# FP32 decoder trunk on one core: the down projection's residual added by accumulating transfers, its subtractions and first evictions on other engines, and the last norm in a written order

## The chip, the cores and the metric

The kernel runs on one core of one Trainium2 chip. The metric is the device time of one execution in microseconds; the number given is the median of three runs. Every text below says TensorE for the matrix engine, VectorE (DVE in the rows), ScalarE (ACT), GpSimd (POOL) and SyncE (SP, which only starts transfers).

## What is computed

A two-layer decoder trunk over 1024 tokens of width 1024, in float32: one recurrent layer, one sparse-attention layer, each followed by a gated feed-forward part, and a last norm. Cut to what the change touches:

```python
def rmsnorm(x, g):
    y = x * lax.rsqrt(jnp.mean(x * x, axis=-1, keepdims=True) + EPS)
    return y * g

def swiglu(h, w_gu, w_down):
    u = h @ w_gu                      # 1024 -> 2 * 2816
    return (jax.nn.silu(u[..., :D_FF]) * u[..., D_FF:]) @ w_down

for layer in range(2):
    h = h + mixer(rmsnorm(h, norm_g[layer, 0]))
    h = h + swiglu(rmsnorm(h, norm_g[layer, 1]), w_gu[layer], w_down[layer])
return rmsnorm(h, final_g)
```

## The kernel before, in words

Activations are held transposed: eight tiles h[0] to h[7] of 128 features by 1024 tokens. Every float32 product is made of three products of split operands: a number is split into a rounded high part (ScalarE copy, L231) and the rest (VectorE subtraction, L232), and high x high, high x low and low x high are summed in PSUM. So each operand of TensorE costs one ScalarE and one VectorE operation before it can be used.

The feed-forward part (`ffn`, L681) multiplies 2x2 blocks with seven block products in place of eight (a Strassen-like scheme); sums of blocks of weights are made by transfers that add into SBUF (`acc`, L189, issued on GpSimd's queue, L190), sums of activations by GpSimd subtractions. The gated part goes over a list `seq` of block products, 12 matmuls each, evicted by `evict`. The norm of its input is applied late: `rstd_a` (L270) gets the reciprocal root per token (matmul of the squares with ones, L274; a power on GpSimd, L279; small VectorE steps, L281 to L285; diagonal matrices `dg`, L298), called at i == 4; `rstd_b` (L304) spreads it over the partitions by a matmul with ones (prb, L310) and a ScalarE copy, called at i == 6. Evictions that need it are held back until then (`late`). Product 6 of the list writes bank b of column tile 0 and is evicted at L791; product 7 is the same for column tile 1; product 8 (block product 7 of tile 0) adds onto bank b of tile 0.

The down projection (`down`, L853, with `block_proj`, L932) runs over three groups of contraction tiles (`DG = [3, 4, 4]`), in each over the seven block products in the order 1, 5, 6, 3, 7, 4, 2 (the text calls them steps), and in each step over four output tiles p: 84 products of 9 or 12 matmuls (L1022). For each product a weight is split (`pump`, L997, up to six products ahead), for each step the operands of the next one are made from the z tiles (`xop`, L945: a GpSimd subtraction at L949 to L955 for steps 5, 6, 4 and 7, then a split), and each product is evicted by adding its bank onto a half of a tile of h on VectorE (L1028). The weights of steps 5, 6, 3 and 7 are made in place in one tile by successive accumulating transfers (`prep`, L967, L991). The tiles of h start as the residual, loaded from DRAM by SyncE, 512 KB each (`hload`, L866, asked for four products ahead).

In the last layer (`last`, `tail`) the squares are summed on GpSimd or VectorE (`sq`, L883), and the last norm (`finish`, L1080) is made for tokens 512 to 1023 while steps 4 and 2 of the last group run, then for tokens 0 to 255 and 256 to 511; for that the last step is cut into two halves of 256 tokens. The outputs are scaled by VectorE (L1092) and sent by ScalarE's and SyncE's queues (L1094).

Which instruction stands where on its engine is decided by the framework's planner, a list scheduler with a timing model of its own, by program order and by the raised priority of a few blocks (`high_priority`). A part under `manual_schedule` keeps the written order instead.

Of the kernel before, what the change touches and what calls it, by code (L numbers as in the profile page):

```python
# [67 lines left out]
class Trunk:  # L68
# [612 lines left out]
    def ffn(self, L, h, last=False):  # L681
# [171 lines left out]
    def down(self, L, hd, zd, zout, last):  # L853
# [12 lines left out]
        def hload(m):  # L866
            h[m] = self.slot("h")
            nc.sync.dma_start(h[m], hd[m])
# [29 lines left out]
        for j, p, c in pr:  # L898
            if last:
                for m, x in {3: ((p, hi),), 7: ((p + 4, hi),), 4: ((p + 4, q[0]), (p + 4, q[1]))}.get(j, ((p, c),) if c else ()):  # L900
                    with self.tc.high_priority(offset=PRIO if j == 2 else 0):
                        sq(m, x, nc.vector if j == 2 else nc.gpsimd)
# [2 lines left out]
                if j == 4 or c == q[0]:
                    next(fin, None)
                if (j, p, c) == (2, 3, q[0]):
                    for _ in fin:
                        pass
                    fin = self.finish(h, st.pop(0), 0, 256)  # L910
                    with self.tc.high_priority(offset=PRIO):
                        next(fin)
            else:
                for m, x in {3: ((p, hi),), 7: ((p + 4, hi),), 4: ((p + 4, lo),), 2: ((p, lo),)}.get(j, ()):
                    kv(m, x)
                if (j, p) == (4, 3):
                    self.ld, self.sp = LD, SP
                    self.wpump(self.wi + 4, self.wi + 2)
        if last:
            next(fin)  # L920
            next(fin)
            f1 = self.finish(h, st.pop(256), 256, 256)
            with self.tc.high_priority(offset=PRIO):
                next(f1)
            for f in (fin, f1):
                for _ in f:
                    pass
            yield h
        else:
            yield kv  # L930
# [1052 lines left out]
```

## Time and profile before

| | before |
|---|---|
| median of three runs | 2741.74 us (2738.09 to 2742.91) |
| the profiled execution's own time | 2742.32 us |
| its span, first to last instruction | 2740.6 us |
| mean granted TensorE clock | 0.988 of full |
| TensorE busy | 2658.2 us, 97% of the span |
| VectorE, ScalarE, GpSimd busy | 69%, 47%, 41% |
| down projection of layer 0, of layer 1 | about 905 to 1122 us, 2485 to 2722 us |

A row of the timeline reads: start in us, busy us, engine, line of the kernel, operation, written tile <- read tiles, shape, count; in brackets the idle time of that engine before it and what ended it. A row that stands for several instructions gives the time they were busy together.

### The profile page before, as it was taken

The page shows a single profiled execution, that of the slowest core. Times are in us where ns is not written, and L with a number is a line of the kernel's source. Part 1 is how long each engine was busy: PE and PEld are TensorE (multiplying, and loading weights), DVE is VectorE, ACT ScalarE, POOL GpSimd, SP SyncE. Part 2 cuts the span into 40 slices and gives each one's busy share as a digit, 9 for nine tenths or more (in the row PEclk, how much of TensorE's full clock was granted, in tenths as well). Part 3 has the DMA queues.
Part 4 walks back from the last instruction along what each step waited for, and adds up shares of the span by engine and source line. Part 5 has one row for each costly group of instructions (what it writes and reads, how often), then busy time and mean ns, then how long its engine had stood idle before and what let it go on. Part 6 is the DMA issues. An engine that isn't in the chain of part 4 may idle for free.

```text
span 2740.6 us, 36687 instructions
## 1 busy us (share of the span) xinstructions
PE 2658.2 (97%) x12650; PEld 2204.7 (80%) x12650; DVE 1892.1 (69%) x3641; ACT 1301.7 (47%) x2505; POOL 1120.5 (41%) x1102
## 2 busy tenths in 40 slices
PE   8989999999999999999999999999999999999997
PEld 6867888788888778888888878888887888887786
DVE  8655734755555898647647999999856545557997
ACT  4656622433223443424415888989934323223433
POOL 2431103444333555110004677777634434436552
PEclk9998999999999999999999999999999999999998
DMA  3323533466564975353485322221354666559761
GB/s 126 93 83 104 170 143 111 112 156 166 150 161 117 324 201 112 133 154 91 162 244 155 82 67 59 67 76 49 108 174 104 170 156 152 154 128 287 194 146 62
DMA packets 175178, 377.03 MB, mean 138 GB/s; under 512 B 16896, under 2 KB 66432, under 8 KB 174992
## 3 DMA queue, kind: packets, MB, share of 16 engines
q1 hardware_dynamic: 121232, 256.79, 28.8%
q0 software_dynamic: 51872, 115.43, 19.6%
q10 hardware_dynamic: 1888, 2.46, 0.2%
q8 instruction: 100, 1.64, 0.2%
q14 instruction: 86, 0.70, 0.1%
HBM read 289.68 MB, written 78.64 MB: 134 GB/s over the span
## 4 chain that ended last, share of the span: by engine, by line
PE 68%; DVE 13%; issue 4%; DMA 3%; ACT 2%; POOL 1%; POOLq 0%; DVEq 0%; SPq 0%; ACTq 0%
PE pb L777 13%; PE pc L777 8%; PE pa L777 8%; PE pn L239 7%; PE pU L1022 6%; PE psc L239 4%; PE po L239 4%; DVE so L232 3%; PE pt L1644 2%; PE py L239 2%; PE pV L1022 2%; PE pwo L1834 2%; PE pW L1022 1%; PE po L1682 1%; PE po L1683 1%
## 5 line engine op out<-in xcount | busy, mean ns | idle before, releaser
L232 DVE TENSOR_TENSOR so<-wr,so 128x512 fp32r<-128x512 f32 (+1 forms) x476 | 390.9, 851 | 55.2 <-ACT so L231 54.6
L231 ACT ACTIVATE so<-wr 128x512 fp32r<-128x512 f32 (+1 forms) x476 | 279.1, 611 | 247.1 <-DMA wr<-w_dn 114.3
L777 PE MATMUL pb<-so,so 128*128 128x512 f32 x1584 | 382.8, 392 | 0.7 <-DVE so L232 0.7
L777 PEld LDWEIGHTS pb<-so,so 128*128 128x128 f32 x1584 | 300.2, 190 | 63.6 <-DVE so L232 1.1
L777 PE MATMUL pa<-so,so 128*128 128x512 f32 x1056 | 254.2, 393 | 4.1 <-ACT ev L786 2.6
L777 PE MATMUL pc<-so,so 128*128 128x512 f32 x1056 | 255.6, 389 | 0.0
L190 POOL DMA_DIRECT2D wr<-w_gu x176 | 161.6, 1076 | 226.0 <-DVE so L232 178.9
L1022 PE MATMUL pU<-so,so 128*128 128x512 f32 x1056 | 245.4, 390 | 2.3 <-DVE so L232 2.3
L777 PEld LDWEIGHTS pa<-so,so 128*128 128x128 f32 x1056 | 199.5, 189 | 46.6 <-DVE so L232 2.7
L239 PE MATMUL psc<-kl,ql 96*128 96x512 f32 (+2 forms) x960 | 232.8, 368 | 2.1 <-DVE thl L232 1.2
L1022 PEld LDWEIGHTS pU<-so,so 128*128 128x128 f32 x1056 | 197.9, 188 | 45.3 <-DVE so L232 4.0
L777 PEld LDWEIGHTS pc<-so,so 128*128 128x128 f32 x1056 | 198.3, 188 | 41.1
L805 ACT ACTIVATE ev<-ev 128x512 f32<-128x512 f32 x44 | 27.8, 632 | 349.4 <-POOL ev L804 349.4
L239 PEld LDWEIGHTS psc<-kl,ql 96*128 96x128 f32 x960 | 164.1, 190 | 24.7 <-PE pt L1644 2.2
L190 POOL DMA_DIRECT2D wr<-w_dn x96 | 91.4, 1136 | 135.7 <-DVE so L232 46.1
L804 POOL TENSOR_TENSOR ev<-ev,rb 128x512 f32<-128x512 f32 x44 | 58.2, 1322 | 209.0 <-DVE ev L803 209.0
L232 DVE TENSOR_TENSOR wl<-wr,wh 128x1024 fp32r<-128x1024 f32 (+4 forms) x79 | 87.8, 1127 | 77.5 <-ACT wh L231 53.2
L232 DVE TENSOR_TENSOR thl<-pt,thl 128x512 fp32r<-128x512 f32 x198 | 133.0, 681 | 10.3 <-ACT thl L231 10.1
L1022 PE MATMUL pV<-so,so 128*128 128x512 f32 x528 | 125.0, 392 | 8.6 <-DVE so L232 6.0
L231 ACT ACTIVATE wh<-wr 128x1024 fp32r<-128x1024 f32 (+4 forms) x97 | 90.1, 956 | 77.6 <-DMA wr<-w_q 19.7
L1022 PEld LDWEIGHTS pV<-so,so 128*128 128x128 f32 x528 | 98.2, 188 | 33.4 <-DVE so L232 7.7
L231 ACT ACTIVATE thl<-pt 128x512 fp32r<-128x512 f32 x198 | 114.5, 597 | 20.2 <-PE pt L1644 18.8
(331 smaller groups left out, 6366.7 us busy)
## 6 DMA issues: line engine op xcount, KB each, us to landing
wr<-w_gu SPq DMA_DIRECT2D x110, 512.0 KB, 4.8
wr<-w_gu POOLq DMA_DIRECT2D x176, 256.0 KB, 5.1
zd<-ev SPq DMA_DIRECT2D x44, 512.0 KB, 3.2
zr<-zd SPq DMA_DIRECT2D x44, 512.0 KB, 6.3
wr<-w_dn SPq DMA_DIRECT2D x40, 512.0 KB, 7.2
wr<-w_dn POOLq DMA_DIRECT2D x64, 256.0 KB, 5.1
ql<-qd SPq DMA_DIRECT2D x64, 192.0 KB, 3.1
wr<-w_in SPq DMA_DIRECT2D x23, 512.0 KB, 3.8
```

The source lines that it names most:

```text
L190: self.nc.gpsimd.dma_start(dst, src, accum_op=ALU.add)
L231: nc.scalar.activation(hi, src, AF.Copy)
L232: (nc.gpsimd if pool else nc.vector).tensor_tensor(lo, src, hi.bitcast(F32), ALU.subtract)
L239: self.nc.tensor.matmul(ps, a, b, start=j == 0, stop=j == n - 1)
L777: nc.tensor.matmul(p, a, b, start=k + n == 0 and j in (1, 5, 6), stop=k == 3 and n == 2, skip_group_check=j not in (1, 5, 6))
L804: nc.gpsimd.tensor_tensor(t0[:, hi], t0[:, hi], rb[:, hi], ALU.mult)
L805: nc.scalar.activation(t0[:, hi], t0[:, hi], AF.Silu)
L1022: nc.tensor.matmul(ps, a, b, start=k + n == 0 and j in (1, 5, 2), stop=k == G[g] - 1 and n == 2, skip_group_check=j not in (1, 5, 2))
L1644: nc.tensor.transpose(pt[:, h * P:(h + 1) * P], Pt[n][h][r][:, off:off + P], self.ident)
L1682: nc.tensor.matmul(po[n], v, thl[:, 0:512], start=False, stop=False)
L1683: nc.tensor.matmul(po[n], v, thl[:, 512:1024], start=False, stop=end)
L1834: self.nc.tensor.matmul(p, wk[a], x[b], start=k + j == 0, stop=k == KD - 1 and j == 2)
```

## The change

- Every norm: the Newton step after the power takes three small VectorE operations in place of four.
- Gated part: `rstd_b` and the held-back evictions come at i == 8 in place of i == 6.
- Down projection: `hload` only reserves the tile. The residual is added by 16 accumulating transfers of 256 KB per layer (`hadd`), one after each product of steps 6, 3, 4 and 2 of the second group, each into a half of h that this step does not touch. The first product that reaches a half is copied there by ScalarE (with its sign) in place of being added by VectorE. The four subtractions of `xop` go from GpSimd to VectorE, and a z tile is let go one step earlier.
- Last layer: in the last group the operands and weights of step 2 are made at the start of step 4 (weights two products further ahead). From the end of step 4 on, the order on TensorE, VectorE, ScalarE and GpSimd is written by hand (`tail`): sums of squares on VectorE, the last square added by the ones-matmul itself, four of the eight output tiles scaled by GpSimd from an SBUF copy of the factor (for that ScalarE multiplies h[4] to h[7] by the norm's weight in advance).

```diff
-        nc.vector.tensor_tensor(t, y, y, ALU.mult)
+        nc.vector.scalar_tensor_tensor(t, y, -0.5, y, op0=ALU.mult, op1=ALU.mult)
         nc.vector.tensor_tensor(t, t, v, ALU.mult)
-        nc.vector.tensor_scalar(t, t, -0.5, 1.5, op0=ALU.mult, op1=ALU.add)
-        nc.vector.tensor_tensor(rt, y, t, ALU.mult)
+        nc.vector.scalar_tensor_tensor(rt, t, 1.5, y, op0=ALU.add, op1=ALU.mult)
...
-            if i == 6:
+            if i == 8:
                 st["rb"] = self.rstd_b(dg)
...
         def hload(m):
             h[m] = self.slot("h")
-            nc.sync.dma_start(h[m], hd[m])
+
+        def hadd(m, c):
+            self.acc(h[m][:, c], hd[m][:, c])
...
+        if last:
+            def scale(m, c):
+                nc.scalar.activation(h[m][:, c], h[m][:, c], AF.Copy, scale=self.gvec(5, m))
+            for j, p, c in pr:
+                for m, x in {3: ((p, hi),), 7: ((p + 4, hi),), 4: ((p + 4, q[0]), (p + 4, q[1]))}.get(j, ()):
+                    sq(m, x, nc.gpsimd)
                 if (j, p) == (7, 3):
                     fin = self.finish(h, st.pop(512), 512, 512)
+                if j == 4:
+                    next(fin)
+                    scale(p + 4, hi)
+                if (j, p) == (4, 3):
+                    with self.tc.manual_schedule(engines={getattr(mybir.EngineType, x) for x in TMS.split()}):
+                        self.tail(h, pr, fin, st, scale)
...
+    def tail(self, h, pr, fin, ss, scale):
...
+        def part(u, m):
+            o = outs[u][m // 4][:, (m % 4) * 256:(m % 4 + 1) * 256]
+            if 4 <= m < 7:
+                if u or m == 4:
+                    G.tensor_tensor(o, h[m][:, q[u]], rbs[u][1], ALU.mult)
+                else:
+                    V.tensor_tensor(o, h[m][:, q[u]], rbs[u][0], ALU.mult)
             else:
+                V.scalar_tensor_tensor(o, h[m][:, q[u]], self.gvec(5, m), rbs[u][0], op0=ALU.mult, op1=ALU.mult)
...
+        for p in range(4):
+            next(pr)
+            square(0, p)
+            if p:
+                add(0, p - 1)
+                scale(p + 3, slice(0, 512))
+            next(fin, None)
+        for _ in fin:
+            pass
+        for p in range(2):
+            next(pr)
+            square(1, p)
+        add(1, 0)
+
+        def side():
+            next(pr)
+            square(1, 2)
+            add(1, 1)
+
+        dg = root(sums(0), side)
+        add(1, 2)
+        next(pr)
+        square(1, 3)
+        spread(0, dg)
+        for m in (4, 7, 0):
+            part(0, m)
+        dg = root(sums(1), lambda: part(0, 1))
+        for m in (5, 6, 2, 3):
+            part(0, m)
+        send(0, 4, 4, nc.sync)
+        send(0, 0, 4, nc.sync)
+        spread(1, dg)
+        for m in (4, 0, 5, 1, 6, 2, 3, 7):
+            part(1, m)
+        send(1, 0, 2, nc.sync)
+        send(1, 4, 2, nc.scalar)
...
             if j == 5:
-                nc.gpsimd.tensor_tensor(a[:, lo], a[:, hi], a[:, lo], ALU.subtract)
+                V(a[:, lo], a[:, hi], a[:, lo], ALU.subtract)
...
-                V(h[m][:, c], h[m][:, c], ps, op)
+                if (m, c.start) in fresh:
+                    fresh.remove((m, c.start))
+                    nc.scalar.activation(h[m][:, c], ps, AF.Copy, scale=-1.0 if op == ALU.subtract else 1.0)
+                else:
+                    V(h[m][:, c], h[m][:, c], ps, op)
...
+        adds = {(1, 6): (0, lo), (1, 3): (4, lo), (1, 4): (0, hi), (1, 2): (4, hi)}
         moves = {1: (0, lo, ALU.subtract), 2: (0, lo, ALU.add), 5: (4, hi, ALU.add), 6: (0, hi, ALU.subtract),
                  3: (0, hi, ALU.subtract), 7: (4, hi, ALU.add), 4: (4, lo, ALU.add)}
...
-            pump(i)
+            if tail and (g, o) == (len(G) - 1, 5):
+                pump(i + 2)
+                if p == 0:
+                    for k in range(G[g]):
+                        xop(g, order[6], k)
+            else:
+                pump(i)
...
             product(i)
+            if (g, j) in adds:
+                m, c = adds[(g, j)]
+                hadd(m + p, c)
```

In `tail`, `root(pm, side)` makes the root for 256 tokens (v, power, then `side()`, then three small steps and dg), `sums` the ones-matmuls, `spread` the matmul with ones and ScalarE's copy of the factor. `finish` (tokens 512 to 1023) waits three yields longer and lets GpSimd scale its output tiles 4 to 7.

## Rows read from the trace of the kernel before

**Rows 1.** The page, busy time of each engine over the whole span.

```profile
PE 2658.2 (97%) x12650; PEld 2204.7 (80%) x12650; DVE 1892.1 (69%) x3641; ACT 1301.7 (47%) x2505; POOL 1120.5 (41%) x1102
```

**Rows 2.** Waits of TensorE over the whole span (line, tile, what released it: us in total, times, longest).

```profile
PE prb L310 <- DVE dg L298: 6.9, 2, 4.0
PE prb L1086 <- DVE dg L288: 6.5, 3, 2.3
PE pV L1022 <- DVE so L232: 6.0, 4, 2.0
```

**Rows 3.** Windows of the two down projections, in each layer groups 0 and 1: stretch, its length, then busy us (and count) of TensorE, its weight loads, VectorE, ScalarE and GpSimd, granted clock, busy share of the 16 DMA engines, GB/s.

```profile
905.00:960.00 55.00, 51.54 (x221) 40.63 (x220) 48.30 (x71) 25.87 (x53) 28.93 (x26) 1.00 1.00 317
960.00:1040.00 80.00, 78.13 (x344) 64.09 (x343) 79.90 (x96) 35.24 (x62) 47.35 (x43) 1.00 0.80 205
...
2485.00:2541.00 56.00, 53.00 (x229) 42.26 (x228) 47.58 (x68) 25.47 (x52) 33.64 (x29) 1.00 1.02 309
2541.00:2617.00 76.00, 73.39 (x322) 59.83 (x321) 75.50 (x98) 35.25 (x62) 38.48 (x37) 1.00 0.78 214
```

**Rows 4.** VectorE's groups by form, 2485 to 2640 us (groups 0 and 1 of layer 1): count, busy us, mean ns, idle time before.

```profile
L232 DVE TENSOR_TENSOR so<-wr,so 128x512 fp32r<-128x512 f32 x36 | 50.6, 1405 | 0.1
L232 DVE TENSOR_TENSOR so<-zr,so 128x512 fp32r<-128x512 f32 x38 | 33.0, 869 | 0.0
L1028 DVE TENSOR_TENSOR h<-h,pU 128x512 f32<-128x512 f32 x32 | 21.5, 680 | 0.4 <-PE pU L1022 0.4
```

**Rows 5.** GpSimd's groups by form in the same stretch.

```profile
L190 POOL DMA_DIRECT2D wr<-w_dn x38 | 38.3, 1154 | 59.4 <-DVE so L232 31.4 <-DVE so L959 26.4 <-DVE h L1028 1.5
L955 POOL TENSOR_TENSOR zr<-zr,zr 128x512 f32<-128x512 f32 x11 | 20.3, 1846 | 0.5 <-DMA zr<-zd 0.5
```

**Rows 6.** The chain of waits, 2485 to 2506 us (start, us, what).

```profile
2486.39 17.17 DMA h<-hd
```

**Rows 7.** The page, DMA queues (packets, MB, share of 16 engines over the span; q1 is fed by SP, q0 by GpSimd) and DMA issues (count, KB each, median us from issue to landing).

```profile
q1 hardware_dynamic: 121232, 256.79, 28.8%
q0 software_dynamic: 51872, 115.43, 19.6%
...
wr<-w_dn POOLq DMA_DIRECT2D x64, 256.0 KB, 5.1
...
h<-hd SPq DMA_DIRECT2D x16, 512.0 KB, 15.0
```

**Rows 8.** Timeline of the gated part of layer 1 around the spread.

```profile
2090.55 0.17 DVE L281 TENSOR_TENSOR rt<-ry 128x8 f32<-128x8 f32 x1 [1.79 <-POOL ry L279]
...
2092.78 1.22 DVE L298 TENSOR_TENSOR dg<-ident,rl 128x1024 fp32r<-128x1024 f32 x1
...
2092.92 1.22 PE L310 MATMUL prb<-dg,onesr 128*128 128x512 f32 x2 [3.97 <-DVE dg L298]
...
2095.12 0.68 DVE L791 TENSOR_TENSOR ev<-ev,pb 128x512 f32<-128x512 f32 x1
```

**Rows 9.** Timeline of the gated part of layer 0 around the spread.

```profile
508.30 1.12 PE L310 MATMUL prb<-dg,onesr 128*128 128x512 f32 x2 [2.89 <-DVE dg L298]
...
509.30 0.68 DVE L791 TENSOR_TENSOR ev<-ev,pb 128x512 f32<-128x512 f32 x1
```

**Rows 10.** Windows of 2 us after these waits (columns as above; the clock is the figure after the last engine).

```profile
508.00:510.00 2.00, 1.70 (x4) 1.40 (x5) 2.00 (x4) 0.00 (x0) 0.00 (x0) 0.61 0.55 94
510.00:512.00 2.00, 2.00 (x6) 1.56 (x5) 2.00 (x4) 0.00 (x0) 0.00 (x0) 0.53 0.00 0
...
2094.00:2096.00 2.00, 2.00 (x6) 1.61 (x5) 2.00 (x4) 0.00 (x0) 0.00 (x0) 0.50 0.00 0
```

**Rows 11.** ScalarE's copies of a bank from PSUM (duration ns min/median/max, first and last start, form).

```profile
L786 ACT ACTIVATE ev<-pa x44: 574/598/600, 490.7 to 2472.4; 128x512 f32<-128x512 f32 x44
```

**Rows 12.** Timeline of the end, layer 1.

```profile
2703.20 1.43 POOL L891 TENSOR_TENSOR ss<-ss,sq 128x256 f32<-128x256 f32 x2 [0.41 <-ACT sq L890]
...
2706.25 1.74 PE L1086 MATMUL prb<-dg,ones 128*128 128x512 f32 x2 [1.89 <-DVE dg L288]
...
2707.00 13.50 PE L1022 MATMUL pW<-so,so 128*128 128x256 f32 x96
...
2714.01 1.08 DVE L1028 TENSOR_TENSOR h<-h,pW 128x256 f32<-128x256 f32 x3 [1.89 <-PE pW L1022]
2714.53 1.08 ACT L890 ACTIVATE sq<-h 128x256 f32<-128x256 f32 x3 [8.26 <-DVE h L1028]
...
2716.66 1.40 DVE L1092 SCALAR_TENSOR_TENSOR out<-h,cv,prb 128x512 f32<-128x512 f32 x2
...
2723.18 0.71 POOL L279 TENSOR_TENSOR ry<-rv,mhalf 128x2 f32<-128x2 f32 x1 [14.13 <-DVE rv L277]
...
2724.70 0.43 DVE L288 TENSOR_TENSOR dg<-ident,rtok 128x256 f32<-128x256 f32 x1
2725.05 2.01 DVE L891 TENSOR_TENSOR ss<-ss,sq 128x256 f32<-128x256 f32 x4
...
2725.19 1.22 PE L1086 MATMUL prb<-dg,ones 128*128 128x256 f32 x2 [2.29 <-DVE dg L288]
...
2730.26 6.35 DVE L1092 SCALAR_TENSOR_TENSOR out<-h,cv,prb 128x256 f32<-128x256 f32 x16
```

**Rows 13.** Window of 2 us inside the W products.

```profile
2711.00:2713.00 2.00, 2.00 (x19) 2.00 (x19) 1.12 (x2) 0.00 (x0) 0.00 (x0) 1.00 0.57 218
```

More of the change, by code (lines that the diff above doesn't have):

```diff
@@ L46 @@
 XA = 3
+TMS = "PE DVE Activation Pool"
 C_G = 0
@@ L872, in down @@
                              [f"d{L}_{g}" for g in range(len(DG))], [self.d["w_dn"][L, g] for g in range(len(DG))],
-                             (1, 5, 6, 3, 7, 4, 2), last)
+                             (1, 5, 6, 3, 7, 4, 2), hadd, last)
         next(pr)
@@ L897, in down @@
         q = [slice(0, 256), slice(256, 512)]
[L898 to L902, printed above, removed]
+        if last:
[4 more added lines that the diff above has]
+                    sq(m, x, nc.gpsimd)
@@ L903, in down @@
                 if (j, p) == (7, 3):
                     fin = self.finish(h, st.pop(512), 512, 512)
[L905 to L912, printed above, removed]
-            else:
[L914 to L930, printed above, removed]
-    def block_proj(self, h, hload, G, xload, wkey, wsrcs, order, tail=False):
+                if j == 4:
+                    next(fin)
+                    scale(p + 4, hi)
@@ new lines, in down @@
+                if (j, p) == (4, 3):
+                    with self.tc.manual_schedule(engines={getattr(mybir.EngineType, x) for x in TMS.split()}):
+                        self.tail(h, pr, fin, st, scale)
+            yield h
+            return
+        for j, p, c in pr:
+            for m, x in {3: ((p, hi),), 7: ((p + 4, hi),), 4: ((p + 4, lo),), 2: ((p, lo),)}.get(j, ()):
+                kv(m, x)
+            if (j, p) == (4, 3):
+                self.ld, self.sp = LD, SP
+                self.wpump(self.wi + 4, self.wi + 2)
@@ L933, in block_proj @@
+    def block_proj(self, h, hload, G, xload, wkey, wsrcs, order, hadd, tail=False):
         nc = self.nc
@@ L963, in xop @@
             X.setdefault((g, j), []).append(t)
+            if j == 4:
+                raw[g][k] = None
             if j == order[6]:
-                raw[g][k] = raw[g][G[g] + k] = None
+                raw[g][G[g] + k] = None
         def prep(i):
@@ L1035, in product @@
                 del X[(g, j)]
+        fresh = {(m, c0) for m in range(KD) for c0 in (0, 512)}
+        adds = {(1, 6): (0, lo), (1, 3): (4, lo), (1, 4): (0, hi), (1, 2): (4, hi)}
         moves = {1: (0, lo, ALU.subtract), 2: (0, lo, ALU.add), 5: (4, hi, ALU.add), 6: (0, hi, ALU.subtract),
@@ L1066, in block_proj @@
             product(i)
+            if (g, j) in adds:
+                m, c = adds[(g, j)]
+                hadd(m + p, c)
             ng, nj = (g, order[o + 1]) if o < 6 else (g + 1, order[0])
-            if ng < len(G) and p < G[ng]:
+            if ng < len(G) and p < G[ng] and not (tail and (g, o) == (len(G) - 1, 5)):
                 xop(ng, nj, p)
@@ L1082, in finish @@
         dg, _ = self.rstd_a(ss, wd // P)
-        yield
-        yield
+        for _ in range(5):
+            yield
         pb = self.ps("prb")[:, 0:wd]
```

66 lines of the change are left out of this document (58 added, 8 removed).

## The prediction

> **What bounds the kernel now.** I read the share of each engine first: TensorE is busy 97% of the span [rows 1], so only two things can pay: stretches where TensorE idles, and the end, where nothing is left for it. The table of its waits comes next. Inside the code that the diff touches they are the spread of the norm's factor in the gated part (prb L310, 6.9 us in two waits), the down projection (pV L1022 on VectorE's splits, the largest of several), and the last norm (prb L1086, 6.5 us) [rows 2]. The windows of the two down projections size the second: TensorE idles 3.46 + 1.87 us in layer 0 and 3.00 + 2.61 us in layer 1, together 10.9 us [rows 3]. In the same windows VectorE is busy 79.90 of 80 and 75.50 of 76 us while GpSimd works 47 and 38 us.
>
> Why VectorE is full there is in the groups by form: a 128x512 split of a weight (two SBUF operands) takes 1405 ns on average and one of z 869 ns, where an eviction (one PSUM, one SBUF operand) takes 680 ns [rows 4]. The subtractions on GpSimd, 1.8 us each in the row of L955 [rows 5], run beside them. The chain of waits adds a second cause at the head of layer 1: it stands 17.17 us on the load of the residual, for which the first eviction waits with VectorE's queue behind it [rows 6].
>
> **Part 1, the gated part (i == 6 becomes i == 8).** TensorE falls free at 508.30 - 2.89 = 505.41 in layer 0 [rows 9] and at 2092.92 - 3.97 = 2088.95 in layer 1 [rows 8], and waits for dg. The clock then falls from 1.00 to about half (the 1.2 GHz level): 0.61 and 0.53 in two slices of layer 0, 0.50 in one of layer 1 [rows 10]. That loses 1.6 us in layer 0, and some 3 us in layer 1 with the edges of those slices (an estimate). So the whole stall is worth 2.89 + 1.6 + 3.97 + 3 = 11.5 us, the upper end. Two more products (12 matmuls at 73.39 / 322 = 0.228 us, 2.73 us each [rows 3]) now go ahead of the spread. The second of them, (0,7), adds onto the bank of (0,6), so it waits until evict (0,6), L791, has read it; and in VectorE's order L791 stands behind dg [rows 8, 9]. With that order kept and one small operation less in the root (0.2 us, an estimate), layer 0 has product 7 until 508.14 and L791 done at 509.30 + 0.68 - 0.2 = 509.8: 1.65 us of idle time for 2.89, and perhaps half of the slow clock, a gain of 2. In layer 1 product 7 ends at 2091.68 and L791 at 2095.6: 3.9 us idle for 3.97, a gain of 0 to 1. I take 3 us for both. The lower end is -1.3: the two held-back evictions (0.68 us each at VectorE's rate) now stand before that of (0,7), which (0,4) needs. In the other norms a shorter root is hidden under products and counts nothing; uncovered it would give 0.2 us each.
>
> **Part 2, the down projections.** Per layer: 44 subtractions leave GpSimd for VectorE, 44 x 0.68 = 29.9 us by the unstretched operation; 16 first evictions leave it for ScalarE, 10.9 us off VectorE and 16 x 0.60 = 9.6 us onto ScalarE, by its copy from PSUM [rows 11], which is idle half of the time. What GpSimd no longer does to VectorE is, in 2485 to 2640 us alone, 36 x (1405 - 680) + 38 x (869 - 680) ns = 33.3 us [rows 4]. So VectorE ends 33.3 + 10.9 - 29.9 = 14 us lighter per layer. The 8 loads of the residual leave SP and the crowded head; 16 adds of 256 KB come to GpSimd's queue in group 1, 16 x 1.15 = 18.5 us of issuing [rows 5] against up to 44 x 1.85 = 81 us of subtractions less. Queued behind an add are the weights' accumulates. Each add touches a half of h that was last written at least 8 products (22 us) earlier and is next written 8 or more later, against 5.1 us to land, so it neither waits nor is waited for. In DMA time: the hardware queue took 0.288 x 2740.6 / 256.79 = 3.07 us per MB, the software queue 0.196 x 2740.6 / 115.43 = 4.65 [rows 7]; 4.19 MB are 12.9 us less at the head and 19.5 us more in group 1. Over 2485 to 2617 us the engines were busy 57 + 59 of 132 us [rows 3]; that becomes 123 of 132. It fits, but only if group 1's own loads move forward into the room at the head. That is why of the 10.9 us I take 7. Ends: 10.9, all idle time gone; on the other side a loss, which is priced as the slower rival D.
>
> **Part 3, the tail.** Time zero is when TensorE has finished the products of step 4: 2706.25 - 1.89 = 2704.36 [rows 12]; the span ends 36.2 us later. Before: 1.89 us idle, the spread, a clock at half for the first W products (96 matmuls in 13.50 us, where 19 take 2.00 us at full clock [rows 12, 13]), then for the last quarter VectorE adds squares only after the other quarter's root (x4 at 2725.05), and 16 outputs come in one row at the end, 6.35 us.
>
> After, in the written order: W(0) and W(1) take 12 x 0.105 = 1.26 us each; the spread comes at 2.5, its dg being ready at 1.9; the other two first halves end near 6.0, the next two at 8.5. VectorE has evictions, sums (0.36 to 0.50 each) and four 512-wide outputs (0.70 each) until 10.9. Sum 0 by matmul is done by then; v 11.1, power on GpSimd (0.71) 12.0, small steps and dg 13.1, spread (1.22) 14.3. Last eviction 13.9, its square (0.4) 14.4, sum 1 15.5, v and power 16.4, dg 17.5, spread 18.8, ScalarE's copy 19.3. Then five outputs on VectorE (0.40 each) beside three on GpSimd (0.72 each): 21.6. From the last output, 2730.26 + 6.35 = 2736.6, to the end were 4.0 us, for issue and landing: end at 25.6. The gain is at most 36.2 - 25.6 = 10.6 us. Hidden beside this: ScalarE's scalings, the first half's outputs, the sends; without cover the three GpSimd outputs cost 2.2 us in series. I take 8.5, because VectorE's and GpSimd's operations of two SBUF operands stretch each other here too [rows 4]; the lower end is 2, if VectorE is still splitting W's operands when the section begins.
>
> **Sum.** 3 + 7 + 8.5 = 18.5 us. The profiled execution took 2742.3 us (span 2740.6), 0.6 above the runs' median of 2741.7, so the forecast for the median is 2723 us.
>
> **Rivals.**
> B: the planner puts evict (0,6) ahead of dg. Then product 8 runs in the gap and the whole 11.5 us of part 1 goes: 2723 - 8.5 = 2714.5. For it: VectorE idles 1.79 us before the root in layer 1 while GpSimd computes the power [rows 8], room for an eviction. Against it: the order on record in both layers [rows 8, 9].
> C: the down projections' waits only move, from VectorE to the transfers: 123 of 132 us of DMA time leaves 9. Part 2 gives 1: 2729.
> D, slower: the adds delay the weights. Place: group 1, steps 6 and 3, where a tile can take its next accumulate only after the split of the step before, 4 products (10.9 us) earlier. That chain is 0.68 + 1.15 + 5.1 + 0.6 + 0.68 = 8.2 us, so 2.7 us are spare. Were the accumulates to land in 15.0 us, as the residual's loads did [rows 7], two steps in each layer lose 7.2 us: 29 us, against 8.5 + 3 + 6.5 (the idle time of the two heads) gained: 2752. It decides once a landing passes 5.1 + 2.7 + 18 / 4 = 12.3 us. Against it: those 15.0 us were under a DMA share of 1.02, and group 1 stood at 0.78 [rows 3].
> The Trainium skill's page "DMA: Bandwidth & Descriptors" ("Issuing engines are not separate DMA queues" and "SWDGE vs HWDGE vs iDMA") speaks for D: all issuers end on the same 16 engines, and the software path has one queue, so an add stands in line with the accumulates. The same page's fit for one software DMA, 2.0 us + bytes / 436e3, would land 256 KB in an estimated 2.6 us and make the spare time of that chain 5.2 us; the trace's 5.1 us differs and is what the sum uses.
> E: the hand order does little (VectorE enters it with a backlog): part 3 gives 2, the time is 2729.5.
>
> **Chances.** Forecast 0.50, B 0.18, C 0.20, D 0.06, E 0.06. Range 2712 to 2735: it holds B, C and E with the bounds of part 3, and leaves out D and the sum of all upper ends (2709). About 0.2%, 5.5 us, is what a measurement of this kernel can tell. Faster 0.86; same 0.08 (low ends of C and E together); slower 0.06 (D).
>
> **What would show it.** Right: no wait of prb L310 above 2 us in layer 0, but a new one of the next product on L791, above 3 us in layer 1; in the down projections splits near 700 ns, VectorE busy under 90% and TensorE's idle time under 4 us in all; the adds landing in 5 to 8 us; from the end of step 4's products to the end of the span 26 to 30 us. Wrong: splits still above 1 us with no GpSimd subtraction left; waits of ScalarE on w_dn longer than before in group 1; TensorE standing before the first W product.

## The result, and the profile after

The changed kernel takes 2717.99 us (median of 4 runs, 2715.61 to 2718.91) against 2740.9 for the kernel before in the same comparison: a ratio of 0.9916, 95% interval 0.9899 to 0.9933, so 22.9 us less where 18.5 were forecast. The profiled execution took 2718.13 us, with a span of 2716.3. In the code after, the lines read L777 (gated products), L1116 (down products, L1022 before), L1126 (evictions, L1028), L232/L233 (split, L231/L232), L191 (adds and accumulates, L190), L949 to L981 (the end).

Each execution was cut at landmarks taken from the products' own rows: first gated product, first product of the down projection, its last product, end of step 4, end of the span. The landmarks are good to 0.2 us. "Rest" is all in front of layer 0's gated part and between the layers, where nothing was changed.

| us | gated 0 | down 0 | gated 1 | down 1 to step 4 | end | rest |
|---|---|---|---|---|---|---|
| before | 428.5 | 222.4 | 424.6 | 212.8 | 36.2 | 1415.7 |
| changed | 424.1 | 215.8 | 423.2 | 205.4 | 30.2 | 1417.4 |
| difference | -4.4 | -6.6 | -1.4 | -7.4 | -6.0 | +1.7 |
| forecast | -2 | -3.5 | -1 | -3.5 | -8.5 | 0 |

(The forecast of 7 us for both down projections is halved here.)

The engines' shares on the page say little: TensorE 98% instead of 97% [rows 1].

```profile
PE 2655.8 (98%) x12658; PEld 2207.0 (81%) x12658; DVE 1837.5 (68%) x3680; ACT 1323.4 (49%) x2547; POOL 1038.2 (38%) x1054
```

The waits of TensorE over the whole span say more. The spread's wait in the gated part is down from 6.9 us in two to 2.1 in one, the 6.0 us of the down projections on VectorE's splits are gone, and 0.6 us on ScalarE is all that TensorE still waits there [rows 2].

```profile
PE prb L963 <- DVE dg L957: 3.6, 2, 2.2
...
PE prb L310 <- DVE dg L298: 2.1, 1, 2.1
...
PE pb L777 <- DVE ev L791: 1.2, 2, 0.7
...
PE prb L1195 <- DVE dg L288: 1.0, 1, 1.0
...
PE pV L1116 <- ACT so L1050: 0.6, 1, 0.6
```

The windows of the down projections, with the columns of [rows 3], and as the last row layer 1's whole stretch to the end of step 4:

```profile
905.00:960.00 55.00, 54.40 (x239) 44.43 (x238) 47.40 (x81) 31.60 (x64) 18.49 (x21) 1.00 0.91 259
960.00:1040.00 80.00, 80.00 (x354) 66.24 (x354) 67.92 (x112) 36.91 (x65) 30.14 (x35) 1.00 0.98 237
2475.00:2531.00 56.00, 55.90 (x245) 45.53 (x245) 48.63 (x78) 33.69 (x69) 18.86 (x19) 1.00 0.93 267
2531.00:2607.00 76.00, 76.00 (x337) 62.93 (x336) 66.28 (x109) 34.56 (x60) 30.16 (x37) 1.00 0.97 245
2480.50:2686.10 205.60, 205.50 (x909) 169.55 (x908) 170.19 (x270) 101.75 (x191) 66.03 (x70) 1.00 0.72 179
```

TensorE has next to no idle time left there (0.6 us in the first window, 0.1 in the third), VectorE is at 85 to 87% in group 1 instead of 99%, and the transfers' share went from 0.78 and 0.80 to 0.97 and 0.98. Why VectorE has room is in its groups, 2475 to 2630 us: both splits cost what an eviction costs, where they took 1405 and 869 ns [rows 4].

```profile
L233 DVE TENSOR_TENSOR so<-zr,so 128x512 fp32r<-128x512 f32 x42 | 29.9, 712 | 2.6 <-ACT so L232 2.6
L233 DVE TENSOR_TENSOR so<-wr,so 128x512 fp32r<-128x512 f32 x40 | 27.4, 687 | 13.2 <-ACT so L232 13.0
...
L1126 DVE TENSOR_TENSOR h<-h,pU 128x512 f32<-128x512 f32 x20 | 13.6, 682 | 0.6 <-PE pU L1116 0.5
```

The price is in the landing times of GpSimd's transfers, as the page's lists of queues and issues show: 7.8 us for an accumulate where it was 5.1, and 8.7 for an add [rows 7].

```profile
q1 hardware_dynamic: 119472, 248.92, 28.3%
q0 software_dynamic: 56480, 123.82, 21.2%
...
wr<-w_dn POOLq DMA_DIRECT2D x64, 256.0 KB, 7.8
...
h<-hd POOLq DMA_DIRECT2D x32, 256.0 KB, 8.7
```

At the spread in layer 1, products 6 and 7 run ahead of the spread, where only product 6 did, and product 8 comes behind it; TensorE waits 2.07 us for dg and then 0.67 for L791, 2.7 us in all instead of 3.97 [rows 8]:

```profile
2083.73 1.22 DVE L298 TENSOR_TENSOR dg<-ident,rl 128x1024 fp32r<-128x1024 f32 x1
...
2083.87 2.36 PE L310 MATMUL prb<-dg,onesr 128*128 128x512 f32 x4 [2.07 <-DVE dg L298]
...
2086.07 0.68 DVE L791 TENSOR_TENSOR ev<-ev,pb 128x512 f32<-128x512 f32 x1
2086.90 3.32 PE L777 MATMUL pb<-so,so 128*128 128x512 f32 x7 [0.67 <-DVE ev L791]
```

The end, from 2686.1 us (the end of step 4) on, in the timeline [rows 12]: small steps of the root, beside them six additions of squares on GpSimd, the spread, the outputs of the 512-token norm, the power of the next root, the last spread, the last outputs.

```profile
2686.73 4.63 POOL L893 TENSOR_TENSOR ss<-ss,sq 128x256 f32<-128x256 f32 x6
2686.78 0.71 DVE L282 SCALAR_TENSOR_TENSOR rt<-ry 128x4 f32<-128x4 f32 x1 [0.56 <-POOL ry L280]
2687.52 0.66 DVE L283 TENSOR_TENSOR rt<-rt,rv 128x4 f32<-128x4 f32 x1
...
2690.15 1.13 PE L1195 MATMUL prb<-dg,ones 128*128 128x512 f32 x2 [0.97 <-DVE dg L288]
...
2694.84 5.31 POOL L1205 TENSOR_TENSOR out<-h,rb 128x512 f32<-128x512 f32 x4 [3.48 <-ACT rb L1198]
...
2700.11 0.89 POOL L950 TENSOR_TENSOR ry<-rv,mhalf 128x2 f32<-128x2 f32 x1
...
2706.29 1.22 PE L963 MATMUL prb<-dg,ones 128*128 128x256 f32 x2 [2.24 <-DVE dg L957]
...
2706.96 3.47 SPq L981 DMA_DIRECT2D outT<-out  x4
2708.01 2.10 POOL L973 TENSOR_TENSOR out<-h,rb 128x256 f32<-128x256 f32 x3 [2.82 <-ACT rb L965]
```

And the last windows of 2 us: the transfers, still at 1.01 in 2700 to 2702 us with the outputs of tokens 512 to 1023, are all but empty from 2704 to 2708 and then full for 6 us, with next to no engine at work in the last 4 of them.

```profile
2704.00:2706.00 2.00, 0.04 (x1) 0.00 (x0) 1.48 (x7) 0.00 (x0) 0.94 (x2) 0.80 0.00 0
2706.00:2708.00 2.00, 1.22 (x2) 0.50 (x2) 1.71 (x6) 0.38 (x1) 0.00 (x0) 0.50 0.05 17
2708.00:2710.00 2.00, 0.00 (x0) 0.00 (x0) 2.00 (x5) 0.00 (x0) 1.99 (x3) 0.50 1.00 344
2710.00:2712.00 2.00, 0.00 (x0) 0.00 (x0) 0.01 (x1) 0.00 (x0) 0.10 (x1) 0.50 1.01 333
2712.00:2714.00 2.00, 0.00 (x0) 0.00 (x0) 0.00 (x0) 0.00 (x0) 0.00 (x0) 0.50 1.00 341
```

### The profile page after: what moved, and what is told of

Read it like the earlier page. It is cut to its first block, busy times and chain, and to the rows that moved or that the text cites. A ratio compares the mean times of both kernels' runs of the same rounds, so it can differ in the third digit from the quotient of the medians.

```text
span 2716.3 us, 36649 instructions
## 1 busy us (share of the span) xinstructions
PE 2655.8 (98%) x12658; PEld 2207.0 (81%) x12658; DVE 1837.5 (68%) x3680; ACT 1323.4 (49%) x2547; POOL 1038.2 (38%) x1054
## 4 chain that ended last, share of the span: by engine, by line
PE 73%; DVE 9%; issue 4%; ACT 2%; DMA 2%; POOL 1%; POOLq 0%; SPq 0%; DVEq 0%; ACTq 0%
PE pb L777 12%; PE pc L777 8%; PE pa L777 8%; PE pU L1116 7%; PE pn L240 7%; PE psc L240 4%; PE pV L1116 4%; PE po L240 4%; PE pt L1758 3%; PE py L240 2%; PE pwo L1948 2%; PE pW L1116 2%; PE po L1796 2%; PE po L1797 2%; DVE so L233 1%
## 5 line engine op out<-in xcount | busy, mean ns | idle before, releaser
L777 PE MATMUL pb<-so,so 128*128 128x512 f32 x1584 | 381.5, 391 | 2.4 <-DVE so L233 1.2
L232 ACT ACTIVATE so<-wr 128x512 fp32r<-128x512 f32 (+1 forms) x476 | 280.0, 612 | 212.5 <-DMA wr<-w_dn 83.0
L233 DVE TENSOR_TENSOR so<-wr,so 128x512 fp32r<-128x512 f32 (+1 forms) x476 | 329.9, 723 | 68.8 <-ACT so L232 68.1
L777 PEld LDWEIGHTS pb<-so,so 128*128 128x128 f32 x1584 | 298.4, 189 | 66.1 <-DVE so L233 1.7
L777 PE MATMUL pa<-so,so 128*128 128x512 f32 x1056 | 254.5, 393 | 2.4 <-DVE so L233 1.4
L777 PE MATMUL pc<-so,so 128*128 128x512 f32 x1056 | 255.6, 389 | 0.0
L191 POOL DMA_DIRECT2D wr<-w_gu x176 | 160.9, 1070 | 239.5 <-DVE so L233 184.1
L1116 PE MATMUL pU<-so,so 128*128 128x512 f32 x1056 | 244.2, 389 | 0.0
L777 PEld LDWEIGHTS pa<-so,so 128*128 128x128 f32 x1056 | 200.0, 190 | 45.1 <-DVE so L233 2.3
L777 PEld LDWEIGHTS pc<-so,so 128*128 128x128 f32 x1056 | 198.2, 188 | 41.1
L1116 PEld LDWEIGHTS pU<-so,so 128*128 128x128 f32 x1056 | 198.1, 188 | 41.1
L191 POOL DMA_DIRECT2D wr<-w_dn x96 | 91.0, 1193 | 148.9 <-DVE so L233 84.7
L233 DVE TENSOR_TENSOR wl<-wr,wh 128x1024 fp32r<-128x1024 f32 (+4 forms) x79 | 87.8, 1127 | 80.4 <-ACT wh L232 56.2
L804 POOL TENSOR_TENSOR ev<-ev,rb 128x512 f32<-128x512 f32 x44 | 59.4, 1351 | 215.6 <-DVE ev L803 215.3
L233 DVE TENSOR_TENSOR thl<-pt,thl 128x512 fp32r<-128x512 f32 x198 | 133.0, 681 | 9.9 <-ACT thl L232 9.4
L232 ACT ACTIVATE wh<-wr 128x1024 fp32r<-128x1024 f32 (+4 forms) x97 | 90.0, 956 | 81.2 <-DMA wr<-w_q 20.8
L232 ACT ACTIVATE thl<-pt 128x512 fp32r<-128x512 f32 x198 | 114.8, 598 | 20.1 <-PE pt L1758 19.2
L1116 PE MATMUL pV<-so,so 128*128 128x512 f32 x528 | 122.7, 390 | 0.7 <-ACT so L1050 0.6
L1116 PEld LDWEIGHTS pV<-so,so 128*128 128x128 f32 x528 | 98.8, 188 | 22.7 <-ACT so L1050 1.0
```

What stands on the lines that cost most here:

```text
L191: self.nc.gpsimd.dma_start(dst, src, accum_op=ALU.add)
L232: nc.scalar.activation(hi, src, AF.Copy)
L233: (nc.gpsimd if pool else nc.vector).tensor_tensor(lo, src, hi.bitcast(F32), ALU.subtract)
L777: nc.tensor.matmul(p, a, b, start=k + n == 0 and j in (1, 5, 6), stop=k == 3 and n == 2, skip_group_check=j not in (1, 5, 6))
L804: nc.gpsimd.tensor_tensor(t0[:, hi], t0[:, hi], rb[:, hi], ALU.mult)
L1116: nc.tensor.matmul(ps, a, b, start=k + n == 0 and j in (1, 5, 2), stop=k == G[g] - 1 and n == 2, skip_group_check=j not in (1, 5, 2))
```

## The experiments

Theory and rivals. The down projections gave twice what was forecast: because the subtractions left GpSimd (S), because the residual left the head (R), or because of both together? The gated part: does the index do it? The end gave less: is it the first microseconds after step 4 or the sending of the outputs? The numbers of all kernels stand here once, stages as above; every ratio is against the kernel before in the same comparison.

| kernel | median | ratio [95%] | gated 0 + 1 | down 0 | down 1 | end |
|---|---|---|---|---|---|---|
| e1 | 2741.08 | 1.0001 [0.9992, 1.001] | 848.4 | 226.0 | 218.5 | 30.1 |
| e2 | 2724.76 | 0.9942 [0.9927, 0.9957] | 848.9 | 219.6 | 209.9 | 29.8 |
| e3 | 2734.9 | 0.9982 [0.9972, 0.9991] | 851.4 | 219.7 | 209.9 | 35.9 |
| e4 | 2720.09 | 0.9922 [0.9905, 0.9938] | 847.5 | 214.9 | 204.8 | 34.0 |
| e5 | 2720.14 | 0.9928 [0.9912, 0.9945] | 849.6 | 215.0 | 204.8 | 30.0 |
| e6 | 2721.28 | 0.9931 [0.9916, 0.9946] | 846.5 | 216.6 | 206.8 | 31.0 |
| e7 | 2716.62 | 0.9914 [0.9899, 0.9929] | 846.2 | 215.1 | 205.1 | 30.3 |
| e8 | 2717.35 | 0.9917 [0.9902, 0.9931] | 845.2 | 215.2 | 205.5 | 29.4 |
| e9 | 2713.47 | 0.9902 [0.9886, 0.9919] | 846.8 | 215.4 | 205.0 | 29.3 |
| e10 | 2714.99 | 0.9908 [0.9893, 0.9923] | 846.1 | 215.0 | 204.8 | 29.9 |
| e11 | 2718.65 | 0.9921 [0.9907, 0.9936] | 848.7 | 215.6 | 204.8 | 30.4 |
| e12 | 2727.2 | 0.9946 [0.9932, 0.996] | 848.7 | 219.3 | 208.7 | 30.4 |

**e1: the changed kernel, subtractions back on GpSimd.**

```diff
-                V(a[:, lo], a[:, hi], a[:, lo], ALU.subtract)
+                nc.gpsimd.tensor_tensor(a[:, lo], a[:, hi], a[:, lo], ALU.subtract)
...
```

> The changed kernel with the four subtractions of the down projection back on GpSimd, the rest kept. Theory S (GpSimd's subtractions stretch VectorE's splits, and that cost the waits): most of the 14 us of both down projections come back, 2728 to 2732 us for 2718, the 128x512 splits of weights above 1.2 us again. Theory R (the residual's loads at the crowded head cost them): within 3 us of 2718, because the loads stay away; the splits may be long, but without waits of TensorE.

Measured: the whole gain is gone, and the two down projections are even 3.6 and 5.7 us longer than before. GpSimd's groups, 2485 to 2640 us:

```profile
L191 POOL DMA_DIRECT2D wr<-w_dn x36 | 51.1, 1643 | 33.0 <-DVE so L233 24.2 <-DMA wr<-w_dn 8.2 <-PE pU L1116 0.6
L191 POOL DMA_DIRECT2D h<-hd x16 | 27.7, 1813 | 21.1 <-DVE h L1126 21.1
L1046 POOL TENSOR_TENSOR zr<-zr,zr 128x512 f32<-128x512 f32 x9 | 22.0, 2548 | 0.9 <-DMA zr<-zd 0.9
```

a group of VectorE's in the same stretch, and all engines in 40 us of group 1:

```profile
L233 DVE TENSOR_TENSOR so<-wr,so 128x512 fp32r<-128x512 f32 x33 | 37.1, 1128 | 6.8 <-ACT so L232 6.8
...
2549.00:2589.00 40.00, 36.17 (x148) 29.20 (x147) 40.00 (x33) 13.46 (x24) 40.00 (x36) 0.91 1.01 198
```

and TensorE's waits in layer 1's down projection, 2480 to 2705 us:

```profile
PE pV L1116 <- DVE so L233: 4.8, 2, 3.8
PE pV L1116 <- ACT so L232: 2.0, 1, 2.0
PE pU L1116 <- DVE so L233: 1.1, 1, 1.1
```

The adds fill GpSimd's queue: from 2549 to 2589 us it works without a gap, on 36 instructions, and VectorE, as full, gets only 33 operations done, 1.2 us each. TensorE's longest wait, 3.83 us, ends at 2578.08, inside this stretch. The longer rows (an accumulate's issue 1643 ns for 1154, a subtraction 2548 for 1846 [rows 5]) are not what an instruction costs in the queue, because the rows of GpSimd overlap: those of 2548 to 2589 us add up to 90.9 us. Where one follows directly on another, an issue takes 0.78 us from its start to the next start and a subtraction 1.47, against 0.69 and 1.37 before. One expectation failed: splits of weights took 1128 ns on average, under the 1.2 us that S named and under the 1405 of before. The splits of z were longer, 971 ns for 869. How the loss divides between stretched operations and late accumulates isn't shown.

**e2: the changed kernel, the residual loaded by SyncE as before; no adds, no first copies.**

```diff
+            nc.sync.dma_start(h[m], hd[m])
...
-            self.acc(h[m][:, c], hd[m][:, c])
+            pass
...
-        fresh = {(m, c0) for m in range(KD) for c0 in (0, 512)}
+        fresh = set()
```

> The changed kernel with the residual loaded at the head by SyncE as before, no adds by transfer and no first copies on ScalarE; the subtractions stay on VectorE. Theory S: within 4 us of 2718, splits near 0.7 us. Theory R: 8 to 14 us come back, 2726 to 2732 us, with TensorE's idle time at the head of each down projection near 3 us as before.

**e3: the kernel before, with only the subtractions moved to VectorE.**

```diff
-                nc.gpsimd.tensor_tensor(a[:, lo], a[:, hi], a[:, lo], ALU.subtract)
+                V(a[:, lo], a[:, hi], a[:, lo], ALU.subtract)
...
```

> The kernel before with the subtractions of the down projection on VectorE and nothing else changed. Theory S: 10 to 14 us faster than before, 2727 to 2731 us. Theory R: within 3 us of before, 2738 to 2744 us. If both causes are needed to remove a wait: 4 to 9 us, 2732 to 2737.

In e3 the splits of weights cost what an eviction costs, so moving the subtractions is enough for that (2480 to 2625 us; [rows 4] has 1405 ns):

```profile
L232 DVE TENSOR_TENSOR so<-wr,so 128x512 fp32r<-128x512 f32 x37 | 25.2, 682 | 0.0
```

The four combinations of the two edits, as changes of down 0 / down 1 against before: neither, 0 / 0; subtractions alone (e3) -2.7 / -2.9; adds with the subtractions on GpSimd (e1) +3.6 / +5.7; both -6.6 / -7.4. So neither S nor R holds by itself: S alone gives 5.6 of 14.0 us, R alone costs 9.3, and R on top of S gives 8.4. (e2 and e3 differ in every other edit and agree to 0.1 us here, so the rest of the change does nothing in these stages without R. R itself is three things: loads that are gone, adds, and first evictions on ScalarE; e6 below puts 2.2 us to the last.) What S leaves standing is at the head, as the timeline of VectorE and of TensorE in layer 0 of e2 shows (e3 has the same shape, 2.66 us on the load and 2.7 on TensorE):

```profile
921.90 0.69 DVE L1127 TENSOR_TENSOR h<-h,pV 128x512 f32<-128x512 f32 x1 [2.76 <-DMA h<-hd]
...
927.37 2.93 PE L1117 MATMUL pU<-so,so 128*128 128x512 f32 x6 [2.51 <-DVE so L233]
```

An eviction that needs the residual stands on its load, the splits for the next product are queued behind it, and the granted clock after the wait was 0.91 over 920 to 940 us.

**e4: the changed kernel with the end of the kernel before** (also its `finish` and its order of `pump` in the last step).

```diff
-                if (j, p) == (4, 3):
-                    with self.tc.manual_schedule(engines={getattr(mybir.EngineType, x) for x in TMS.split()}):
-                        self.tail(h, pr, fin, st, scale)
+                if (j, p, c) == (2, 3, q[0]):
+                    for _ in fin:
+                        pass
+                    fin = self.finish(h, st.pop(0), 0, 256)
...
```

> The changed kernel with the end of before: the planner's order, the last norm as it was, step 2's operands made at their old place; the gated part and the down projections stay changed. If the written order brings what its stage shows (36.2 us from the end of step 4 to the end before, 30.2 after): 6 us slower than 2718, 2724. Rival, the planner's own order gains from the freed GpSimd and VectorE too: at most 2 us slower, 2718 to 2720.

Measured: an end of 34.0 us. The order by hand, with its outputs on GpSimd and step 2's operands made early, is worth 3.8 of the 6.0 us of the end; the other 2.2 came with the rest of the change. In e4's trace v of the first of the last two roots comes 16.8 us after the end of step 4, where it came 18.5 us after it (18.2 in e3), and each of the two roots is 0.2 us shorter from v to dg. The medians, 2.1 us apart, can't tell the two expectations apart: 2720.09 is next to the rival's 2718 to 2720, and the stage alone separates them.

**e5: the changed kernel with the old index. e6: the changed kernel with its first copies on VectorE.**

```diff
-            if i == 8:
+            if i == 6:
```

```diff
-                    nc.scalar.activation(h[m][:, c], ps, AF.Copy, scale=-1.0 if op == ALU.subtract else 1.0)
+                    nc.vector.tensor_scalar(h[m][:, c], ps, -1.0 if op == ALU.subtract else 1.0, None, op0=ALU.mult)
```

> The changed kernel with the spread of the norm's factor and the held-back evictions at i == 6 again. If moving them is what shortened the gated parts (layer 0 from its first product to the first product of the down projection 428.5 us before, 424.1 after; layer 1 424.6 and 423.2): 3 to 6 us slower, 2721 to 2724, with a wait of TensorE on dg of 2 to 4 us in each layer. Rival: the gated parts gained by chance of the clock and of an earlier wait (on L786): within 2 us of 2718.

> The changed kernel with the first copy of each half made by VectorE (a multiplication by 1 or -1 from PSUM) in place of ScalarE. Theory: VectorE has room (170 of 206 us busy in the down projection of layer 1), 16 copies of 0.68 us per layer cost at most 2 us in all. Rival: VectorE is what limits the head (group 0): 3 to 6 us slower, with waits of TensorE on splits there.

In e5 the wait for dg is back, 1.4 and 3.8 us; its two gated parts are 849.6 us, where the eleven kernels with a later spread lie between 845.2 and 848.9 (mean 847.3), so the index is worth some 2.3 us, less than the 3 to 6 expected. That is one profile against eleven which are 3.7 us apart among themselves; the wait shows it better than the sum. e6 loses 0.8 + 1.4 us in the down projections and 0.8 at the end; its median is 3.3 above the changed kernel's. VectorE has 9 us more work in each layer (189.35 against 180.39, 179.25 against 170.19) and covers most of it.

**e7: the root one eviction later** (rival B's order, VectorE evicts (0,6) ahead of dg). **e8: the outputs of tokens 0 to 255 sent in three parts.**

```diff
-            if i == 4:
-                dg, _ = self.rstd_a(ss)
-            if i == 8:
+            if i == 10:
...
+            if i == 6:
+                dg, _ = self.rstd_a(ss)
```

```diff
+        send(0, 0, 2, nc.sync)
-        for m in (5, 6, 2, 3):
+        for m in (5, 6):
             part(0, m)
...
-        send(0, 0, 4, nc.sync)
+        for m in (2, 3):
+            part(0, m)
...
+        send(0, 2, 2, nc.scalar)
```

> The changed kernel with the root of the gated part's norm asked for after evict (0,6) (i == 6) and spread at i == 10, so that VectorE evicts bank b of tile 0 ahead of the root. If the order of L791 and dg is what the two products still wait for (waits on dg 2.1 us and on L791 1.2 us in all, and a clock at half behind them): both waits go, 3 to 6 us faster than 2718, 2712 to 2715. Rival: the root is late instead and TensorE waits for it at its new place: 2718 to 2722.

> The changed kernel with the outputs of tokens 0 to 255 sent in three parts, tiles 0 and 1 as soon as they are scaled, tiles 2 and 3 on ScalarE's queue. The last 2 MB leave together (DMA share 1.00 from 2708 to 2714 us, 0.19 from 2702 to 2706): if the end is bound by these transfers, the stretch from the end of step 4 to the end of the span falls from 30.2 to 29.0 to 29.5 us. Rival: it is bound by the last operation and the latency of one transfer: 30 us or more.

e7 leaves no wait for dg, but the evictions of a bank take its place. The waits of TensorE in layer 0, 478 to 545 us:

```profile
PE pa L777 <- ACT ev L786: 2.1, 1, 2.1
PE pb L777 <- DVE rv L278: 1.3, 1, 1.3
PE pa L777 <- DVE so L233: 1.2, 1, 1.2
PE pb L777 <- DVE ev L791: 0.9, 1, 0.9
```

That is 5.5 us against 3.8 in the changed kernel; in layer 1 (2058 to 2130 us, changed 2057 to 2130) 3.8 against 3.1. Rival B's 8.5 us are not to be had by this order. e8's end is 0.8 us shorter: the transfers have a share of 0.38 in the 2 us that end 21.5 us after the end of step 4, where the changed kernel has 0.05 until 21.9, but after that they are near full again (0.99 from 2707 to 2709).

**e9: e7 and e8 together**, and **e11: e8, and two of GpSimd's outputs moved behind the power of the next root**:

```diff
-        for k0 in (4, 0, 6, 2):
+        for k0 in (4, 0, 2, 6):
...
-        for _ in fin:
-            pass
+        next(fin)
...
         dg = root(sums(0), side)
+        for _ in fin:
+            pass
```

> The changed kernel with two edits that each showed no measurable difference: the root of the gated part's norm issued at product 6, after that product's eviction, and its spread at product 10 (VectorE then evicts (0,6) ahead of dg, which is the order that rival B supposed); and the outputs of tokens 0 to 255 sent in three parts. If both gain what their stages showed (1.4 us in the gated part of layer 1, 0.6 us at the end), the median is 2715 to 2717; if the first only moves the waits from dg to the evictions, it is 2716.5 to 2718.5, and TensorE's waits from 478 to 545 us add up to 5 to 6 us.

> The changed kernel with the outputs of tokens 0 to 255 sent in three parts as they come free (as in the run before that did this), and the last two of GpSimd's outputs of the 512-token norm issued after the power of the next root instead of ahead of it. If the power stood behind GpSimd's outputs (1.05 us from rv to its start in the changed kernel): ry starts within 0.3 us of rv, the factor of tokens 0 to 255 comes 1 us sooner, and the last products' end to the end of the span is 28 to 29 us (changed 30.2; sends alone 29.6). Rival: VectorE's queue of outputs and evictions sets the pace, so the factor comes sooner but the last output does not: 29.3 to 30. The median is then 2715.5 to 2718 and can't tell the two; the stage can.

e9 has the lowest median of all, with an interval that overlaps the changed kernel's. Its median is also below both expectations, while TensorE's waits from 478 to 545 us add up to 5.4, as the second one said. The stages of the table are 2.2 us shorter together, 1.4 of it in the two that the edits touch (gated parts and end); the unchanged rest of its profiled execution was 3.2 us shorter as well, and that rest varies between 1414.2 and 1420.9 over all profiles, so e9 is not shown to be faster. e11's end is 30.4 us, beyond both expectations. The power did start 0.23 us after rv, but the small steps behind it then met the outputs:

```profile
2696.95 0.71 POOL L950 TENSOR_TENSOR ry<-rv,mhalf 128x2 f32<-128x2 f32 x1 [1.81 <-DVE rv L949]
2697.63 2.62 POOL L1209 TENSOR_TENSOR out<-h,rb 128x512 f32<-128x512 f32 x2
2697.81 1.24 DVE L953 SCALAR_TENSOR_TENSOR rt<-ry 128x2 f32<-128x2 f32 x1
2699.08 1.19 DVE L954 TENSOR_TENSOR rt<-rt,rv 128x2 f32<-128x2 f32 x1
2700.30 0.16 DVE L955 SCALAR_TENSOR_TENSOR rtok<-rt,ry 128x2 f32<-128x2 f32 x1
```

Three steps on two elements a partition: 1.24 and 1.19 us while GpSimd multiplies (two multiplies, 2.62 us together), 0.16 when it has ended. dg came 17.0 us after the end of step 4, in the changed kernel 15.9. The Trainium skill's page "SBUF — State Buffer" ("Who interferes with whom") says that a VectorE instruction with two SBUF inputs contends with a GpSimd instruction that reads SBUF; one with at most one does not, outside two modes of its own. The trace agrees: here, and in the splits' 1405 to 687 ns against the evictions' 680 and 682.

**e10 and e12: eight copies of 512 KB in DRAM beside the changed kernel, which nobody waits for**, to tell the wait for the residual's load from the crowding that it makes.

```diff
+            nc.sync.dma_start(hx[m], hd[m])
```

```diff
+            nc.sync.dma_start(hx[m], zd[zl[m % 2]])
```

> The changed kernel with eight copies of 512 KB, from the residual in DRAM to a scratch tensor in DRAM, issued by SyncE where the kernel before loaded the residual. They move through the same queue and nobody waits for them. Theory W (what the residual's load costs at the head of a down projection is the wait of the first eviction, with VectorE's splits queued behind it): no wait of pU on so above 1 us, first pU to last product 214 to 217.5 us in layer 0 and 205 to 207 in layer 1, median within 2 us of the changed kernel, 2716 to 2720. Rival H (the load costs because it crowds the head's transfers, so that z and the weights come late): TensorE waits for a split or a transfer at 915 to 935 us, both down projections are 3 us or more longer (219 and 208.5 or more), median 2723 to 2727.

> The changed kernel with eight copies of 512 KB from DRAM to a scratch tensor in DRAM, issued by SyncE at the head of each down projection. Their source is a tile of z that is written at about 864 to 885 us, so this time they can't run ahead of the head; six of the eight stand in SyncE's queue ahead of the loads of z, which is more crowding than the residual's loads made, and nobody waits for them. Theory W (the residual's load costs by the wait of the first eviction for it, with VectorE's queue behind): TensorE does not wait for a split at 915 to 935 us, down projections of 214 to 218 us (layer 0) and 205 to 207.5 us (layer 1), median 2715 to 2720. Rival H (the load costs by crowding z and the weights): TensorE waits over 2 us in the first 30 us of each down projection or just ahead of it, the two down projections are together 6 us or more longer than 215.8 + 205.4, median 2723 or more. If SyncE's queue delays the z loads by the copies' issue alone (8 x 0.5 us), that is 4 us at most in the wait of ScalarE and VectorE for z, inside the second.

e10 told nothing of the head: its copies waited for no buffer and went out at 367 to 484 us and at 1992 to 2062. They cost nothing that could be measured there, in stretches where the changed kernel's transfers had a share of 0.35 and 0.48. In e12 they lay at 865 to 896 us and the like in layer 1, and the median rose by 9.2 us: down 0 and 1 are 3.5 and 3.3 us longer. By the numbers named in advance that is rival H. But the shape is another one than e2's. There, the loads of z landed in 10.9 us (median of the six at the head; before 10.9, changed 10.8) and TensorE had its first wait at 924.9 us, on the splits behind the eviction; in e12 z landed in 12.7 us, and the first products themselves waited (0.76 us until 902.95, on a ScalarE copy of z). So transfers put ahead of z do cost; that e2's and e3's loss is the wait rests on their own traces, where z is not late. Crowding by copies behind z, as the residual's loads lay, wasn't tried, so what crowding adds to the wait in e2 and e3 isn't shown.

## Why the prediction was right, and where it was off

**The bound** was as read: VectorE, held by GpSimd's subtractions, and the head. The forecast case happened: dg stays ahead of L791, the transfers fit, the end is shorter. That the sum came out within 5 us is in part luck: part 2 gave 7.0 us more than forecast, and the end's 2.5 less took some of it back.

**Part 1** (forecast 3). The two gated parts lost 5.8 us between the two profiles, and e5 puts some 2.3 us of that to the index. The idle time at the spread fell further than worked out: 2.89 to 0.5 (on L791) in layer 0, where 1.65 had been worked out, and 3.97 to 2.7 in layer 1, where it was 3.9. The wait of product 8 on L791 was 0.67 us, where "above 3 us" had been named as the sign: the spread's own matmuls (2.36 us) stand between dg and that product and cover the eviction, which the step had left out. Only product 7 went ahead of the spread, not two products.

**Part 2** (forecast 7, measured 14.0) is the term that was mis-sized; "of the 10.9 us I take 7" fails at the 10.9, called there "all idle time gone". Undisturbed, TensorE takes 205.60 / 909 = 0.2262 us for a matmul in the row of layer 1 above. As many matmuls took 213.2 us before: 7.6 us lost, where the stretch's busy column shows 5.65 idle:

```profile
2491.20:2704.40 213.20, 207.55 (x909) 169.11 (x907) 194.23 (x242) 90.64 (x169) 111.52 (x98) 1.00 0.65 173
```

In layer 0, 948 matmuls make 214.4 of 222.4 us: 8.0 lost. So 15.6 us were there, not 10.9 (over these whole stretches the idle column has 5.32 and 5.65), and 1.4 are left. A matmul's row lasts 389 ns, its pace is 226: the 0.16 us by which the last one before a stall outlasts the pace count as busy, 2.3 us at the 14 stalls that show. Another 18 delays, starts 340 to 390 ns apart, lie wholly inside a row and make 2.1 us. The [rows 3] had it in their counts, 344 matmuls in 80 us where 354 fit. The relief of VectorE was also larger than the 14 us per layer of the step: 194.23 to 170.19 us in layer 1. The step priced only the two forms in [rows 4]; L959's and the 384-wide splits were stretched as well (869 to 748 and 717 to 593 ns). Its 1.15 and 1.85 us for GpSimd's work in [rows 5] were means of rows that overlap, as in e1, and too high; nothing hung on it in the changed kernel. The adds do wait in GpSimd's queue, against "it neither waits": 53.6 us in 16 waits for the eviction ahead of them, up to 17.5 us. TensorE lost nothing by it. The reserve that was kept back for the transfers wasn't needed: 125.8 of 132 us in the two groups of layer 1 (forecast 123), and accumulates landed at 7.8 us, below the 12.3 at which rival D decides. The adds landed at 8.7 us, just past the 5 to 8 named. Rival C's mechanism is there, longer landings, but not its price: ScalarE's waits on w_dn fell from 114.3 to 83.0 us over the span.

**Part 3** (forecast 8.5, measured 6.0; the end at 30.2 us, where 25.6 had been worked out and 27.7 forecast). "I take 8.5, because two-operand operations stretch each other here too" named the right cause and undersized it. The last output ended at 2710.1, 24.0 us after the end of step 4 instead of 21.6. The first spread came 4.0 us after it instead of 2.5, with root steps of 0.71 and 0.66 us beside GpSimd's six additions of squares; and the power stood 1.05 us behind GpSimd's 512-wide outputs of 1.33 us each, which the step had not priced. The other 2.2 us are a step that failed: "from the last output to the end were 4.0 us, for issue and landing". It was 6.2, since the 2 MB of tokens 0 to 511 leave together, 2708 to 2714 us, at a share of 1.00 and some 340 GB/s. In the kernel before, they left while the 16 outputs were being made, and the 4.0 us held only the last of them:

```profile
2734.00:2736.00 2.00, 0.00 (x0) 0.00 (x0) 2.00 (x6) 0.00 (x0) 0.00 (x0) 0.50 0.98 323
```

e8 gives 0.8 back.

**Rival B** gives no 8.5 us even with its order built in (e7). **E** is out by e4. The errors of the three parts (+2.8, +7.0, -2.5) less 1.7 us of unchanged rest make 5.6; the two spans differ by 24.3 us, 5.8 more than the forecast sum.

What stays open: how much of the gated parts' 5.8 us beyond the index is the shorter root and how much is the spread of one profile to the next (e3, with the old index and the old root, has 851.4 us where before had 853.1); how e1's loss divides; and whether crowding has a part in what e2 and e3 lose at the head.

## What to carry to other kernels

Size what a stall can give back by the pace (count times the undisturbed interval), not by the idle column. Before an engine gets more in its queue, ask what already stands there, and which engine it slows: the adds cost 9 us with the subtractions on GpSimd and gave 8 without them. And at an end where nothing follows, count the bytes that leave after the last output becomes known, as well as the last instruction.

## What the runs showed of the hardware

Operations on 2 or 4 elements a partition suffer beside GpSimd like wide ones: 0.16 us alone, up to 1.24 beside a 128x512 multiply of 1.31, about the length of that multiply (e11). Rows of GpSimd overlap when its queue is full, so their mean is no price: 90.9 us of rows in 41.2 us (e1). And 8.4 MB of copies in stretches with free transfer time cost nothing that could be measured (e10), while as many copies ahead of the heads went with a median 9 us higher (e12).
